# A four-layer diffusion backbone on one core: the first FFN products behind both mixers read unnormalised x, and the norm's root is applied to their results

## The chip, the core and the metric

The kernel runs on one NeuronCore of a Trainium2 chip. TensorE (PE) multiplies matrices into PSUM, VectorE (DVE) and ScalarE (ACT) work on tiles of up to 128 partitions in SBUF and PSUM, GpSimd (POOL) on tiles in SBUF, and DMA queues bring weights from HBM. Each engine works through its own instruction stream in order and waits on semaphores. The metric is the device time of one execution in microseconds; lower is better. Before the change it is 1661.69 us, the median of three runs (1661.11 to 1663.94).

## The reference

There are 256 latent tokens (`x`) and 256 context tokens (`ctx`), each 1024 wide, and two layers. A layer is a half FFN, a token mixer and a second half FFN; the mixer of layer 0 is a 2-D Fourier mixing, that of layer 1 a bidirectional retention. In the last layer the context ends with the mixer, so the second FFN of layer 1 works on latent tokens alone.

```python
def rmsnorm(x, g):
    y = x * rsqrt(mean(x * x, axis=-1, keepdims=True) + 1e-6)
    return y * g
def modulate(h, shift, scale):
    return h * (1 + scale) + shift
def swiglu(h, w_gate, w_up, w_down):
    return (silu(h @ w_gate) * (h @ w_up)) @ w_down          # 1024 -> 2816 -> 1024
def half_ffn(t, m, j):
    h = modulate(rmsnorm(t, norm_g[l, j]), m[3 * j], m[3 * j + 1])
    return t + 0.5 * m[3 * j + 2] * swiglu(h, w_gate[l, j // 2], w_up[l, j // 2], w_down[l, j // 2])
# layer: t = half_ffn(t, m, 0); t = t + m[5] * mixer(modulate(rmsnorm(t, g1), m[3], m[4])); t = half_ffn(t, m, 2)
```

The nine vectors `m` of a layer come from `silu(c) @ ada_w[l] + ada_b[l]`, once for the latent tokens and once for the context tokens. With r the root of a token (the reciprocal square root above), `h @ w = r * ((x * g * (1 + scale)) @ w) + shift @ w`. All data is fp32.

## The kernel before, in words

Everything is held transposed: features on partitions, tokens along the free axis. The model width is eight tiles of 128 features (`d` or `k` = 0 to 7); a tile's free axis is 512 tokens, of which 0 to 255 are latent (stream 0) and 256 to 511 context (stream 1). `xlat` and `xctx` hold the residual streams.

**Products.** A matrix product in near-fp32 precision is three single-pass products of split operands. Each operand is written as hi + lo (ScalarE casts hi, VectorE subtracts to get lo: `split`, L88 to L92), and `mm3` (L130 to L134) issues hi*hi, hi*lo, lo*hi into one PSUM accumulation. In the names of the profile `h` is the normalised and modulated input of an FFN or a mixer (sixteen tiles: hi and lo of eight), `wh` and `wl` are the halves of a weight block, `raw` is a block as it comes from HBM, `ps` is one of six PSUM banks and `aux` one of two more. One FFN block of 1024 x 256 weights (128 columns of gate and 128 of up) is 48 products; 22 blocks make the hidden layer, in three chunks, each followed by its share of the down projection.

**The norm.** As each tile of the residual stream is finished (`residual`, L369), ScalarE squares it (L271), and GpSimd or VectorE adds the squares up (L278). `rstd` (L297) then forms one stream's roots: products with a single column sum over partitions (L303), ScalarE takes the square root (L308), VectorE the reciprocal (L310) and a diagonal matrix (L312), and one product spreads the roots over all partitions as a row (L319). `norm_mod` (L327) makes h from it, per tile: VectorE x * scale * root (L335), ScalarE hi with the shift added (L336), VectorE lo (L337). Both read the root from PSUM.

**The two places.** Behind the Fourier mixer (`fourier`, its last loop) and behind the retention (`project_out` of the last head) the latent stream's norm must be complete before the first FFN product can be issued. `keep_warm` (L245) puts products of a constant matrix (L250) at three points of this chain. After that `begin_two` (L1084) starts the FFN of both streams: block 0 and block 1 on the 256 latent columns alone, while the context's norm is formed, then both blocks on the context columns, and from block 2 on all 512 columns at once. `begin_narrow` (L1108) starts the last FFN, which has latent columns only, with blocks 0 and 1.

**The order of the work.** The program is written as one sequence; a scheduler of the framework moves instructions within it by its own estimates, under `tc.issue_after` constraints. Within an engine the resulting order is fixed, so an instruction that waits holds up all that stand behind it on its engine.

## Time and profile before

| What | Value |
|---|---|
| Median of three runs | 1661.69 us |
| The profiled execution's own time | 1660.66 us |
| Its span, first to last instruction | 1658.6 us |
| Mean granted TensorE clock | 0.997 |
| TensorE busy | 1632.2 us, 98% of the span |
| VectorE, ScalarE, GpSimd busy | 1128.2, 627.3, 112.5 us |

The profile names instructions by line, engine, operation, result and operands. In its timelines a row holds the start, the duration, the engine, the line, the shapes and a count of equal instructions that follow each other; a bracket tells for how long the engine was idle before and who released it. Instructions of one engine overlap in part, so the step from one start to the next, and not the duration, is what an instruction costs a busy engine. A full-precision (fp32) product is two records, a split one is one.

### The profile page before, as it was taken

To read this page: it belongs to the slowest core of one execution; us is meant where nothing else is said; L and a number is where in the kernel's file an instruction comes from. 1 tells how busy PE (TensorE), PEld (TensorE's weight loads), DVE (VectorE), ACT (ScalarE), POOL (GpSimd) and SP (SyncE) were. 2 spreads that over 40 slices of the span, in tenths; PEclk is the share of its full clock that TensorE was granted. 3 is DMA by queue.
4 is the path that set the end of the run, shared out by engine and by line. 5 is a ranking of instruction groups with operands and counts; after the bars stand their busy time and mean duration, and the time that the engine had idled before them with its cause. 6 is when DMAs were issued, how large, how long until landed. Compare 5 with 4: busy or idle time off the path is not lost.

```text
span 1658.6 us, 23343 instructions
## 1 busy us (share of the span) xinstructions
PE 1632.2 (98%) x9400; PEld 1429.1 (86%) x9400; DVE 1128.2 (68%) x1805; ACT 627.3 (38%) x910; POOL 112.5 (7%) x180
## 2 busy tenths in 40 slices
PE   6999999999999999999999999999999999999998
PEld 4788888889998888888988888888998999999998
DVE  5688888887867776766566767733566757665554
ACT  4522222255542122223442232233574444354443
POOL 0001111112200000001100000001000000000000
PEclk9999999999999999999999999999999999999999
DMA  9675776752235444544144444422233334345551
GB/s 333 248 261 196 258 256 228 244 197 77 77 140 178 167 166 153 194 163 169 68 152 165 156 167 172 171 99 99 77 127 128 127 108 147 128 164 190 169 188 54
DMA packets 59740, 272.04 MB, mean 164 GB/s; under 512 B 7536, under 2 KB 8944, under 8 KB 41968
## 3 DMA queue, kind: packets, MB, share of 16 engines
q1 hardware_dynamic: 40512, 201.86, 34.4%
q0 software_dynamic: 18576, 68.17, 11.6%
q8 instruction: 74, 1.21, 0.3%
q10 hardware_dynamic: 544, 0.52, 0.1%
q14 instruction: 34, 0.28, 0.0%
HBM read 265.27 MB, written 5.24 MB: 163 GB/s over the span
## 4 chain that ended last, share of the span: by engine, by line
PE 97%; DVE 1%; DMA 1%; ACT 1%; issue 0%; SPq 0%; DVEq 0%; ACTq 0%
PE ps L132 31%; PE ps L133 31%; PE ps L134 31%; DMA a<-in_ada_first 1%; PE aux L303 1%; PE ps L764 0%; PE aux L250 0%; PE aux L195 0%; DMA xctx<-in_x 0%; PE ps L839 0%; ACT wh L89 0%; PE aux L319 0%; PE aux L925 0%; DVE xlat L369 0%; PE aux L358 0%
## 5 line engine op out<-in xcount | busy, mean ns | idle before, releaser
L89 ACT CAST wh<-raw 128x1024 fp32r<-128x1024 f32 x344 | 352.4, 1031 | 712.0 <-PE ps L133 625.9
L133 PE MATMUL ps<-h,wh 128*128 128x512 f32 (+1 forms) x1568 | 554.7, 355 | 0.0
L134 PE MATMUL ps<-h,wl 128*128 128x512 f32 (+1 forms) x1568 | 554.0, 355 | 0.0
L132 PE MATMUL ps<-h,wh 128*128 128x512 f32 (+1 forms) x1568 | 549.7, 355 | 2.5 <-ACT h L89 2.5
L90 DVE TENSOR_TENSOR wl<-raw,wh 128x1024 fp32r<-128x1024 f32 x344 | 410.0, 1197 | 180.1 <-ACT wh L89 175.6
L133 PEld LDWEIGHTS ps<-h,wh 128*128 128x128 f32 x1568 | 296.3, 189 | 41.8 <-DVE h L90 0.4
L132 PEld LDWEIGHTS ps<-h,wh 128*128 128x128 f32 x1568 | 293.6, 189 | 44.5 <-ACT h L89 3.1
L222 DVE CUSTOM_DVE_ANT_0 dump<-araw,wide,adab 128x1024 bf16<-128x1024 f32 x256 | 329.4, 1287 | 3.7 <-DMA araw<-in_ada_w 0.4
L134 PEld LDWEIGHTS ps<-h,wl 128*128 128x128 f32 x1568 | 296.2, 189 | 41.0
L132 PE MATMUL ps<-a,wh 128*128 128x512 f32 (+2 forms) x952 | 317.9, 337 | 0.0
L133 PE MATMUL ps<-a,wh 128*128 128x512 f32 (+2 forms) x952 | 317.9, 336 | 0.0
L134 PE MATMUL ps<-a,wl 128*128 128x512 f32 (+2 forms) x952 | 317.6, 336 | 0.0
L133 PEld LDWEIGHTS ps<-a,wh 128*128 128x128 f32 x952 | 180.8, 190 | 18.8
L134 PEld LDWEIGHTS ps<-a,wl 128*128 128x128 f32 x952 | 180.7, 190 | 18.3
L132 PEld LDWEIGHTS ps<-a,wh 128*128 128x128 f32 x952 | 180.1, 190 | 18.6
L439 DVE TENSOR_TENSOR t<-ps,t 128x512 f32<-128x512 f32 (+1 forms) x88 | 54.9, 624 | 175.3 <-PE ps L134 147.8
L213 POOL DMA_DIRECT2D araw<-in_ada_w x128 | 67.9, 531 | 828.9 <-DVE mods L222 777.8
L369 DVE SCALAR_TENSOR_TENSOR xlat<-ps,mods,xlat 128x256 f32<-128x256 f32 x128 | 61.1, 480 | 63.6 <-PE ps L134 63.0
L437 ACT ACTIVATE t<-ps 128x512 f32<-128x512 f32 (+1 forms) x88 | 48.0, 545 | 130.7 <-PE ps L134 125.0
L90 DVE TENSOR_TENSOR a<-t,a 128x512 fp32r<-128x512 f32 (+2 forms) x116 | 69.8, 606 | 2.4 <-ACT a L89 2.0
L89 ACT CAST a<-t 128x512 fp32r<-128x512 f32 (+2 forms) x116 | 64.2, 558 | 12.0 <-DVE t L868 9.1
L278 POOL TENSOR_TENSOR q<-q,q 128x256 f32<-128x256 f32 x40 | 36.9, 940 | 188.9 <-ACT q L271 188.7
(208 smaller groups left out, 1159.6 us busy)
## 6 DMA issues: line engine op xcount, KB each, us to landing
raw<-in_wgu SPq DMA_DIRECT2D x85, 1024.0 KB, 4.8
araw<-in_ada_w POOLq DMA_DIRECT2D x128, 512.0 KB, 3.8
raw<-in_wd SPq DMA_DIRECT2D x32, 896.0 KB, 4.5
raw<-in_ret_in SPq DMA_DIRECT2D x24, 1024.0 KB, 4.8
raw<-in_wd SPq DMA_DIRECT2D x16, 1024.0 KB, 4.8
a<-in_ada_first SPq DMA_DIRECT2D x32, 256.0 KB, 5.2
t<-in_four_w SPq DMA_DIRECT2D x32, 256.0 KB, 5.2
raw<-in_ret_out SPq DMA_DIRECT2D x8, 1024.0 KB, 4.7
```

Source lines behind the costliest of these rows:

```text
L89: mark[6] = nc.scalar.copy(hi, src)
L90: i = (lo_eng or nc.vector).tensor_tensor(lo, src, f32(hi), ALU.subtract)
L132: nc.tensor.matmul(ps, lh, rh, start=start, stop=False)
L133: nc.tensor.matmul(ps, lh, rl, start=False, stop=False)
L134: mark[4] = nc.tensor.matmul(ps, ll, rh, start=False, stop=stop)
L213: nc.gpsimd.dma_start(raw, a["ada_w"][l, m, d])
L222: nc.vector.tensor_tensor_reduce(dump, raw, wide[:, v, :], 1.0, adab[:, l, m, d : d + 1], ALU.mult, ALU.add, mods[l][:, m, d, v : v + 1],)
L278: eng.tensor_tensor(n, sums[s][0], sq, ALU.add)
L303: mark[5] = nc.tensor.matmul(ps[:, t : t + 1], sq[:, t * P : t * P + P], meanw[:, 0:1], start=(i + t == 0), stop=(i == n - 1), skip_group_ ...
L369: mark[0] = nc.vector.scalar_tensor_tensor(x_tile(d, s), ps, mods[l][:, m, d, s : s + 1], x_tile(d, s), ALU.mult, ALU.add)
L437: mark[1] = nc.scalar.activation(sg[:, :width], psg[:, :width], AF.Silu)
L439: nc.vector.tensor_tensor(hf[:, :width], psu[:, :width], sg[:, :width], ALU.mult)
```

## The change

Behind both mixers, the first FFN blocks no longer read normalised tiles for the latent tokens.

As each residual tile d is finished, `Ahead.tile(d)` writes x * g * (1 + scale), without the root, as hi and lo into the latent columns of the FFN's h tiles (ScalarE hi, VectorE lo). Each h tile is two columns wider (`SH = 2`): columns 0 and 1 hold the shift vector, hi and lo, written by GpSimd in `Ahead.open()`. A product over columns 0 to 257 then gives, in one pass, the shift's product (column 0) and the unnormalised products of the 256 latent tokens. When the roots are known, `evict` multiplies columns 2 to 257 by the root row as VectorE moves them out of PSUM, and `gate` adds the shift's product as a bias per partition inside the Silu and the gating product.

The squares of both streams are now all added by GpSimd, down to one tile for each stream, and behind the Fourier mixer the roots of both streams are formed in one chain (`roots`), whose first products stand between the FFN products. The `keep_warm` products and the two separate `rstd` chains at these places go. Behind the Fourier mixer blocks 0 and 1 are computed so for the latent tokens, then both for the context columns, which are normalised as before; behind the retention blocks 0, 1 and 2 are. Meanwhile `norm_mod` overwrites the latent columns with normalised values for the other blocks, once the last unnormalised product has read them.

All h tiles have the new width, so every FFN and mixer product that reads h starts two columns (8 bytes) into its tile.

```diff
     def h_tile():
-        return hpool.tile([P, 512], F32R, tag="h", name=nm("h"))
+        return hpool.tile([P, SH + T2], F32R, tag="h", name=nm("h"))
...
     def h_tiles():
-        return [(h_tile(), h_tile()) for _ in range(ND)]
+        return [(h_tile()[:, SH:], h_tile()[:, SH:]) for _ in range(ND)]
...
@@ fourier, last loop
                 for s in range(2):
                     residual(d, z[:, STREAMS[s]], l, 5, s)
-                    square(d, s, nc.gpsimd, 2)
-                    if d == ND - 1 and s == 0:
-                        sqrt_table()
-                        keep_warm(NW[0], mark[4])
-                        after(0)
-        after(1)
+                    if s == 0:
+                        following.tile(d)
+                for s in (1, 0):
+                    square(d, s)
+        sqrt_table()
...
@@ retention, project_out of the last head
                     if hd == HEADS - 1:
-                        square(d, 0, nc.vector, 2)
+                        following.tile(d)
+                        square(d, 0)
...
+        following.open()
         project_out(HEADS - 1, zts.pop(0))
-        keep_warm(NW[0], mark[4])
-        after(0)
...
+    class Ahead:
...
+        def open(self):
+            need(self.l, 3 * self.j + 1)
+            self.full = [(h_tile(), h_tile()) for _ in range(ND)]
...
+            for d, (hi, lo) in enumerate(self.full):
+                sh = mods[self.l][:, 3 * self.j, d, 0:1].broadcast_to([P, SH])
+                nc.gpsimd.tensor_copy(hi[:, :SH], sh)
+                nc.gpsimd.tensor_tensor(lo[:, :SH], sh, f32(hi[:, :SH]), ALU.subtract)
+
+        def tile(self, d):
+            sc = mods[self.l][:, 3 * self.j + 1, d, 0:1]
+            hi, lo = (t[:, STREAMS[0]] for t in nxt["h"][d])
+            nxt["done"][1].append(nc.scalar.activation(hi, x_tile(d, 0), AF.Copy, scale=sc))
+            mark[0] = nc.vector.scalar_tensor_tensor(lo, x_tile(d, 0), sc, f32(hi), ALU.mult, ALU.subtract)
...
+        def products(self, blk, ps, k):
+            hi, lo = (t[:, : SH + S] for t in self.full[k])
+            for gu in range(2):
+                mm3(
+                    ps[gu][:, : SH + S], wcols(blk, k // 4 * 1024 + gu * 512 + k % 4 * P, P), (hi, lo),
+                    k == 0, k == ND - 1,
+                )
+
+        def evict(self, ps, r):
+            col = spool.tile([P, 2], F32, tag="col", name=nm("col"))
+            v = []
+            for gu in range(2):
+                nc.vector.tensor_copy(col[:, gu : gu + 1], ps[gu][:, 0:1])
+                v.append(q_tile())
+                nc.vector.tensor_tensor(v[gu], ps[gu][:, SH : SH + S], r, ALU.mult)
+            return v, col
+
+        def gate(self, v, col, pair):
+            uh, ul = pair
+            sg = q_tile()
+            mark[1] = nc.scalar.activation(sg, v[0], AF.Silu, bias=col[:, 0:1])
+            hf = q_tile()
+            nc.vector.scalar_tensor_tensor(hf, v[1], col[:, 1:2], sg, ALU.add, ALU.mult)
+            split(uh[:, :S], ul[:, :S], hf)
+
+        def roots(self, n):
+            inv = rstd_tokens(n, 1.0 / D**2)
+            diag = t_tile()[:, : n * S]
...
+            r = aux_tile()
+            for s in range(n):
+                nc.tensor.matmul(r[:, STREAMS[s]], meanw, diag[:, STREAMS[s]], start=True, stop=True)
+            row = q_tile()
+            nc.scalar.copy(row, r[:, :S])
+            return r, row
+
+        def begin_two(self, load, bank, part, hidden):
...
+            for k in range(ND):
+                self.products(blks[0], lat[0], k)
+                if k == 4:
+                    r, row = self.roots(2)
+            nxt["done"] = norm_mod(self.l, self.j, 1, h, r[:, late])
+            with behind(3):
+                first = self.evict(lat[0], row)
+            for k in range(ND):
+                self.products(blks[1], lat[1], k)
+            with behind(ND - 1):
+                second = self.evict(lat[1], row)
+                pre = [load(2)]
+            ctx = [(bank(), bank()) for _ in range(2)]
+            for k in range(ND):
+                for i in range(2):
+                    for gu in range(2):
+                        part(blks[i], ctx[i][gu], gu, (k,), late)
+                if k == 0:
+                    with tc.issue_after(mark[0].ins), tc.issue_after(mark[6].ins):
+                        nxt["done"] = norm_mod(self.l, self.j, 0, h, r[:, :S])
...
+        def begin_narrow(self, load, bank, part, hidden):
...
+            for k in range(ND):
+                self.products(blks[0], lat[0], k)
+                if k == 4:
+                    r, row = self.roots(1)
...
-    fourier(0, 0, prepare(0, 2, T2, True))
-    half_ffn(0, 2, nxt["h"], T2, begin_two, prepare(1, 0, T2))
+    following = Ahead(0, 2)
+    fourier(0, 0, following)
+    half_ffn(0, 2, nxt["h"], T2, following.begin_two, prepare(1, 0, T2))
...
-    retention(1, 0, nxt["h"], late, prepare(1, 2, S, True))
-    half_ffn(1, 2, nxt["h"], S, begin_narrow, finish, scale_out)
+    following = Ahead(1, 2)
+    retention(1, 0, nxt["h"], late, following)
+    half_ffn(1, 2, nxt["h"], S, following.begin_narrow, finish, scale_out)
```

Where the instructions stand now, at three places. Rows give line, operation, result and operands with the buffers' numbers, and the result's shape; in the changed program `mm3` is L134 to L136, the tile's lo L1049, the sums over partitions L360, the spreading product L1088.

**TensorE between the Fourier mixer's last product and the FFN.** Before:

```order
L134 MATMUL ps_4056<-a_3409,wl_4014 128x258
L250 MATMUL aux_4094<-meanw 128x128 x6
L303 MATMUL aux_4117<-meanw,q_4000 128x1 x2
L303 MATMUL aux_4117<-meanw,q_4051 128x1 x2
L303 MATMUL aux_4117<-meanw,q_4090 128x1 x2
L250 MATMUL aux_4130<-meanw 128x128 x5
L319 MATMUL aux_4136<-q_4128,meanw 128x256
L250 MATMUL aux_4138<-meanw 128x128 x5
L303 MATMUL aux_4233<-meanw,q_4005 128x1 x2
L303 MATMUL aux_4233<-meanw,q_4054 128x1 x2
L132 MATMUL ps_4189<-h_4101,wh_4181 128x256
```

Now, at the same place (first rows) and 75 products later, inside block 1 (last rows):

```order
L136 MATMUL ps_4106<-a_3409,wl_4058 128x258
L134 MATMUL ps_4163<-h_3743,wh_4155 128x258
L135 MATMUL ps_4163<-h_3744,wh_4155 128x258
...
L134 MATMUL ps_4166<-h_3751,wh_4173 128x258
L360 MATMUL aux_4207<-meanw,q_4145 128x1 x2
L136 MATMUL ps_4165<-h_3751,wl_4174 128x258
L135 MATMUL ps_4166<-h_3752,wh_4173 128x258
L360 MATMUL aux_4207<-meanw,q_4149 128x1 x2
L136 MATMUL ps_4166<-h_3751,wl_4174 128x258
```

FFN products follow the mixer's last product at once; q_4145 and q_4149 are GpSimd's last sums of squares of the context and the latent stream. The products that spread the roots stand behind the last product of block 1, and the context's products right behind them:

```order
L136 MATMUL ps_4166<-h_3757,wl_4174 128x258
L1088 MATMUL aux_4218<-t_4216,meanw 128x256 x2
L134 MATMUL ps_4345<-h_3743,wh_4155 128x256
L134 MATMUL ps_4346<-h_3743,wh_4155 128x256
L135 MATMUL ps_4345<-h_3744,wh_4155 128x256
```

Before, the context was normalised while block 1 ran on the latent columns; now its first product stands directly behind its roots.

**VectorE at the end of the Fourier mixer, now.** The evictions (L681 to L683), residuals (L371), lo halves (L1049), and the two halves of block 1's weights (L92):

```order
L681 TENSOR_TENSOR t_4135<-ps_4106,t_4120 128x2x128
L682 TENSOR_TENSOR t_4135<-ps_4106,t_4120 128x2x128
L371 SCALAR_TENSOR_TENSOR xlat<-t_4090,mods_126,xlat 128x256
L371 SCALAR_TENSOR_TENSOR xctx_98<-t_4090,mods_126,xctx_98 128x256
L683 COPY t_4135<-ps_4106 128x2
L371 SCALAR_TENSOR_TENSOR xlat<-t_4135,mods_126,xlat 128x256
L371 SCALAR_TENSOR_TENSOR xctx_98<-t_4135,mods_126,xctx_98 128x256
L1049 SCALAR_TENSOR_TENSOR h_3756<-xlat,mods_126,h_3755 128x256
L1049 SCALAR_TENSOR_TENSOR h_3758<-xlat,mods_126,h_3757 128x256
L92 TENSOR_TENSOR wl_4170<-raw_4167,wh_4169 128x1024
L92 TENSOR_TENSOR wl_4174<-raw_4167,wh_4173 128x1024
L367 RECIPROCAL inv_4214<-root_4212 128x4
```

Eight lo halves are new in this stretch; the last two (tiles 6 and 7) stand behind the last residuals.

**TensorE behind the retention, now.** Block 0 begins directly behind the mixer; the sums of squares stand after its 48 products and two of block 1:

```order
L136 MATMUL ps_12686<-h_12479,wl_12682 128x258
L134 MATMUL ps_12687<-h_12465,wh_12693 128x258
L135 MATMUL ps_12687<-h_12466,wh_12693 128x258
L360 MATMUL aux_12741<-meanw,q_12673 128x1 x2
...
L135 MATMUL ps_12687<-h_12478,wh_12697 128x258
L1088 MATMUL aux_12750<-t_12748,meanw 128x256
L136 MATMUL ps_12687<-h_12477,wl_12698 128x258
```

The product that spreads the roots stands 36 products later, and behind it the blocks go on with unnormalised tiles.

More of the change, by code (lines that the diff above doesn't have):

```diff
@@ L32 @@
 GRID_W = 64
+SH = 2
 @with_exitstack
@@ L333, in norm_mod @@
             hi, lo = h[d][0][:, sl], h[d][1][:, sl]
-            with tc.issue_after(done[d - 3].ins) if d > 2 else nullcontext():
+            with tc.issue_after(done[-3].ins) if len(done) > 2 else nullcontext():
                 nc.vector.scalar_tensor_tensor(u, x_tile(d, s), sc, r, ALU.mult, ALU.mult)
@@ L350, in scale_parts, with rstd_tokens @@
         return each
-    def rstd_tokens():
+    def rstd_tokens(n=2, scale=1.0):
         ps = aux_tile()
-        for s in range(2):
+        for s in reversed(range(n)):
             for t in range(2):
@@ L708, in rsqrt_small, with retention @@
         return y
-    def retention(l, slot, h, mid, after):
+    def retention(l, slot, h, mid, following):
         need(l, NMOD - 1)
```

87 lines of the change are left out of this document (62 added, 25 removed).

## The prediction

> **What bounds the kernel now.** I read the page's head and busy times first, then the chain of waits, then TensorE's timeline at the two places of the change.
>
> ```profile
> span 1658.6 us, 23343 instructions
> PE 1632.2 (98%) x9400; PEld 1429.1 (86%) x9400; DVE 1128.2 (68%) x1805; ACT 627.3 (38%) x910; POOL 112.5 (7%) x180
> ...
> PE 97%; DVE 1%; DMA 1%; ACT 1%; issue 0%; SPq 0%; DVEq 0%; ACTq 0%
> ```
>
> TensorE is the bound: 1632.2 of 1658.6 us, and 97% of the chain that ended last. But busy is not useful here, since the constant products of L250 count as busy. So the price of a junction is the time from the mixer's last product to a point where both programs have done the same FFN products, less what these need at the steady step. The timeline of TensorE behind the Fourier mixer:
>
> ```profile
> 427.28 0.28 PE L668 MATMUL ps<-a,a 96*128 96x258 f32 x1
> 430.28 0.28 PE L668 MATMUL ps<-a,a 96*128 96x258 f32 x1
> ...
> 443.84 1.50 PE L250 MATMUL aux<-meanw 128*128 128x128 f32 x12
> 445.18 1.65 PE L303 MATMUL aux<-meanw,q 128*128 128x1 f32 x12
> 448.00 0.67 PE L319 MATMUL aux<-q,meanw 128*128 128x256 f32 x2
> 449.94 1.02 PE L303 MATMUL aux<-meanw,q 128*128 128x1 f32 x8
> 450.82 0.48 PE L132 MATMUL ps<-h,wh 128*128 128x256 f32 x2
> ...
> 474.80 0.40 PE L132 MATMUL ps<-h,wh 128*128 128x512 f32 x1
> ```
>
> The step: 25 products lie between the first two rows, 13 of 258 columns and 12 of 256, in 3.00 us, so 0.12 us each. From 443.84 to 450.82 nothing useful is multiplied. From 443.84 to the first 512-wide product at 474.80 are 30.96 us; blocks 0 and 1, both streams, are 4 x 48 = 192 products or 23.04 us. **Junction 1 costs 7.92 us.** Behind the retention:
>
> ```profile
> 1452.60 1.50 PE L250 MATMUL aux<-meanw 128*128 128x128 f32 x12
> 1454.29 1.47 PE L303 MATMUL aux<-meanw,q 128*128 128x1 f32 x12 [0.19 <-DVE q L278]
> 1456.86 0.67 PE L319 MATMUL aux<-q,meanw 128*128 128x256 f32 x2
> 1457.36 1.28 PE L250 MATMUL aux<-meanw 128*128 128x128 f32 x10
> 1458.64 0.74 PE L132 MATMUL ps<-h,wh 128*128 128x256 f32 x4
> 1459.28 0.39 PE L133 MATMUL ps<-h,wh 128*128 128x256 f32 x1
> 1459.50 0.28 PE L134 MATMUL ps<-h,wl 128*128 128x256 f32 x1
> ```
>
> 6.04 us to the first product, and its first five take 0.86 us (1458.64 to 1459.50) where 0.60 is the steady step: **junction 2 costs 6.30 us.** Together 14.22 us can be touched; the rest of the program keeps its products.
>
> **The change, part by part.** The number and the width of the other products stay. A product of 258 columns costs no more than one of 256, as the mixed step above shows, so 96 of them at junction 1 and 144 at junction 2 are free.
>
> *Junction 2, what stays.* The sum over partitions is now one tile, two rows of L303's kind, four records. Eight records took 0.88 us (449.94 to 450.82), so 0.44. One spreading product took 0.50 (1456.86 to 1457.36). Sum 0.94, gain 6.30 - 0.94 = **5.36 us**. That holds if no wait is left. The lo halves come while the mixer still runs; the last is needed seven tiles of six products, 5 us, after the mixer's end. The sums stand after 50 products, 6.0 us after it. Before, VectorE's last square sum landed at 1454.29, 1.7 us after the mixer's end; GpSimd's adds are slower, but six of the seven can run earlier. I take no wait.
>
> *Junction 1, what stays.* Row sums of two streams: eight records, 0.88 us. Two spreading products, 1.00 us. Then a new wait. The context's first product now stands directly behind the spreading products, so TensorE waits for VectorE's x * scale * root and ScalarE's hi. That wait is seen at junction 2 before, where it is filled with L250: from the end of the spreading product (1457.36) to 1458.64, 1.28 us, and 0.26 of slow start, 1.54. ScalarE's copy of the root row stands ahead of it:
>
> ```profile
> L802 ACT COPY t<-ps 128x256 f32<-128x256 f32 x8 | 3.0, 372 | 1.2 <-DVE t L797 1.1
> 450.36 0.47 DVE L335 SCALAR_TENSOR_TENSOR q<-xlat,mods,aux 128x256 f32<-128x256 f32 x1
> 451.15 0.48 DVE L335 SCALAR_TENSOR_TENSOR q<-xlat,mods,aux 128x256 f32<-128x256 f32 x1
> ```
>
> 0.37 more: 1.9 us. After it VectorE makes a tile in 0.79 us (450.36 to 451.15), while block 0's six products of a tile need 0.72: over six tiles 0.4 us.
>
> *The clock.* L250 held TensorE busy; what does a bare wait cost? The windows of two microseconds, with the granted clock third from the end, and the timeline ahead of them:
>
> ```profile
> 414.92 0.39 PE L132 MATMUL ps<-a,t 128*128 128x256 f32 x1 [0.70 <-ACT t L89]
> 415.14 0.28 PE L133 MATMUL ps<-a,t 128*128 128x256 f32 x1
> 416.23 0.39 PE L134 MATMUL ps<-a,t 128*128 128x256 f32 x1 [0.80 <-DVE t L90]
> ...
> 416.00:418.00 2.00, 1.77 (x11) 1.72 (x12) 1.94 (x9) 0.81 (x3) 0.00 (x0) 0.78 0.00 0
> 418.00:420.00 2.00, 2.00 (x11) 2.00 (x11) 0.86 (x4) 0.79 (x3) 0.00 (x0) 0.50 0.00 0
> 420.00:422.00 2.00, 2.00 (x17) 2.00 (x17) 0.73 (x3) 0.89 (x3) 0.00 (x0) 0.86 0.00 0
> ```
>
> Two waits of 0.70 and 0.80 us, with two products between them, were followed by half the clock: (0.22 + 0.50 + 0.14) x 2 = 1.7 us lost. One wait of nearly the same sum was not:
>
> ```profile
> 48.20 1.66 PE L132 MATMUL ps<-h,wh 128*128 128x512 f32 x6 [1.62 <-ACT h L89]
> ...
> 48.00:50.00 2.00, 1.80 (x7) 1.25 (x8) 2.00 (x4) 2.00 (x5) 0.00 (x0) 1.00 0.99 418
> ```
>
> So the loss sets in somewhere from 1.5 to over 1.6 us. The wait of 1.9 us and the gaps of the pace behind it, 2.3 us, lie above both: I count 1.7 us, and keep 0 as the other end.
>
> The Trainium skill, "TensorE: Matmul & The Clock Gate", section "Why this matters for your kernels", allows more: no idle gaps over about 3 us. By it the sum would be 1.7 us lower; the loss behind 1.5 us at 414 to 416 contradicts it.
>
> *The new work on VectorE.* Eight lo halves fall into the mixer's last loop, where VectorE has no room:
>
> ```profile
> 425.00:446.00 21.00, 21.00 (x179) 21.00 (x177) 20.33 (x44) 12.11 (x27) 9.62 (x10) 1.00 0.43 151
> 445.58 0.48 DVE L369 SCALAR_TENSOR_TENSOR xctx<-t,mods,xctx 128x256 f32<-128x256 f32 x1
> L348 DVE SCALAR_TENSOR_TENSOR h<-xlat,mods,h 128x256 fp32r<-128x256 f32 x8 | 5.7, 716 | 1.1 <-ACT h L347 1.0
> ```
>
> It is busy 20.33 of 21.00 us, and its last residual ends at 446.06. The same instruction (L348) took 716 ns in the mean beside GpSimd's adds; alone the step is 0.40 (two such instructions in 0.79 us, above). So the last lo comes 8 x 0.40 to 8 x 0.72 later, at 449.3 to 451.8; tile 7 needs it at 443.84 + 7 x 0.72 + 0.24 = 449.12. TensorE waits 0.2 to 2.7 us. I take 0.7, near the lower end, since GpSimd is busy in only 9.62 of the 21 us and the earlier lo halves can fill the 0.67 us idle. Block 1's weights (L92, behind it) and the roots' reciprocal come later by the same time and have 5 us of products ahead of them.
>
> ScalarE's eight hi halves lie beside this (12.11 of 21.00 us busy). GpSimd's 32 small shift writes come before its adds, behind 42.78 us of idle (row below). The later normalisation of the latent columns and the gates (some 24 instructions of about 0.40 on VectorE) lie beside block 2's 48 wide products, 11 us. No queue of DMAs gains or loses a transfer, and the modulation steps (L222) keep their places in VectorE's order, though `open` asks for them earlier.
>
> Junction 1 then keeps 0.88 + 1.00 + 1.9 + 0.4 + 1.7 + 0.7 = 6.6 us, gain 7.92 - 6.6 = **1.3 us**. Bounds: without the clock, the late lo and the pace 4.1; with the late lo at 2.7 and a second loss of clock, -2.4.
>
> *The start of h tiles.* All products over h now start 8 bytes into a tile.
>
> ```profile
> L133 PE MATMUL ps<-h,wh 128*128 128x512 f32 x1056 | 411.1, 389 | 0.0
> 499.76 0.39 PE L134 MATMUL ps<-h,wl 128*128 128x512 f32 x1
> 501.34 0.39 PE L132 MATMUL ps<-h,wh 128*128 128x512 f32 x1
> ```
>
> Of the 512-wide ones there are 3 x 1056 = 3168 (this line and its neighbours L132, L134). No row shows such a start. The lower end is 0, since the odd width above cost nothing; the upper what two columns of 512 would be, 0.9 ns of the step (seven from 499.76 to 501.34, 226 ns each), or 2.8 us; I take 0.
>
> **Sum.** 5.4 + 1.3 = 6.7 us off the profiled execution's 1660.66: 1654.0. The median of three runs was 1.0 above that execution, so I predict **1655.0 us**.
>
> **Rivals.** *Sums late.* GpSimd now adds all fourteen squares, in a chain that TensorE meets in the middle of block 1:
>
> ```profile
> 433.12 2.35 DVE L90 TENSOR_TENSOR wl<-raw,wh 128x1024 fp32r<-128x1024 f32 x2
> 433.66 2.40 POOL L278 TENSOR_TENSOR q<-q,q 128x256 f32<-128x256 f32 x1 [42.78 <-ACT q L271]
> L278 POOL TENSOR_TENSOR q<-q,q x40: 729/785/2405, 375.6 to 1180.6; 128x256 f32<-128x256 f32 x40
> ```
>
> An add of 729 ns lasted 2.40 us beside VectorE's two weight halves, and just such a pair (L92) now stands behind the last lo. If four adds are left at its end (lo at 449.8 by the sum, 2.3 for the pair, 0.79 an add), 449.8 + 2.3 + 4 x 0.79 = 455.3, against the row sums' place at 443.84 + 75 x 0.12 + 0.7 = 453.5: 1.8 us more, 1656.8. Beside it, lo halves at their late bound add 2.0: 1657.0. Against it: VectorE's idle moments in the last loop let GpSimd in. The Trainium skill, "SBUF — State Buffer", section "Who interferes with whom", says that a VectorE instruction with two SBUF inputs and a GpSimd one that reads SBUF exclude each other; the 2.40 us row agrees, and by it the wait would be the 1.8 us worked out here.
>
> *The clock stays.* The wait at the context is one piece like that of 1.62 us, not two, and may fall across whatever stretch the clock is judged by: 1655.0 - 1.7 = 1653.3. The rule of the Trainium skill's page on the clock gate, quoted above, speaks for this one.
>
> *Moved, not removed.* Late lo (2.0) and late sums (1.8) together leave 2.9 of the 6.7 us: 1658.8; with a second loss of clock (1.7) 1660.5. For it: both hang on the same full VectorE. Against it: late lo halves also delay block 1, and so give the sums time. No change, by what can be measured.
>
> *Slower.* One mechanism: the shifted start costs each wide product. From 6.7 / 3168 = 2.1 ns each the change gains nothing; were it 16 columns of 512, 7.1 ns, it would be 22.5 us and 1677.5. Against it: the 258-wide products end at an odd place at no cost.
>
> **How the numbers follow.** Forecast 0.37 (1654 to 1656); clock stays 0.25 (1653.3); sums or lo late 0.22 (1657); moved 0.09 (1658.8 to 1660.5); slower 0.05; that the gain at junction 2 is lost in another way 0.02. Two runs of this kernel can be told apart by about 0.2%, 3.3 us. Faster needs 1658.4 or less: 0.84; same 0.10; slower 0.06. Range 1651.8 to 1659.5.
>
> **What would show it.** Right: no L250 at either place, the first FFN product 0.1 to 0.2 us behind the mixer's last, TensorE waiting at the context's first product for ScalarE's hi for about 2 us, a clock of about 0.5 in the next 3 us, and no wait behind the retention. Wrong: a wait of over 1 us at the row sums (L360) on GpSimd's add; waits for L1049's lo over 1 us; a step of the 512-wide products other than 226 ns.

## The result, and the profile after

| | Median | Executions | Lowest to highest |
|---|---|---|---|
| before | 1661.40 us | 4 | 1660.31 to 1663.94 |
| changed | 1675.20 us | 4 | 1674.44 to 1679.17 |

The ratio is 1.0087, with a 95% interval of 1.0075 to 1.0098: the change makes the kernel 13.8 us slower. I had predicted 1655.0 us. The profiled execution is the one of 1679.17 us. Its mean granted clock is 0.994; the other three have 0.998 and spans of 1672.3 to 1673.3 us, so about 4 us of its span are not the change's.

The head of the page after, as before in one line each for span and TensorE:

```profile
span 1677.0 us, 23316 instructions
PE 1647.7 (98%) x9312; PEld 1426.0 (85%) x9312; DVE 1139.4 (68%) x1838; ACT 632.2 (38%) x931; POOL 131.0 (8%) x223
```

TensorE has 88 records fewer than before and is busy 15.5 us longer. Where, the groups by line and shape tell. Of the kernel before (columns behind the shapes: count, busy us, mean ns of one, idle just before):

```profile
L134 PE MATMUL ps<-h,wl 128*128 128x512 f32 x1056 | 410.9, 389 | 0.0
L132 PE MATMUL ps<-h,wh 128*128 128x512 f32 x1056 | 409.8, 390 | 2.5 <-ACT h L89 2.5
L132 PE MATMUL ps<-a,wh 128*128 128x512 f32 x472 | 183.7, 389 | 0.0
L132 PE MATMUL ps<-wh,h 128*128 128x512 f32 x64 | 25.2, 393 | 0.0
L132 PE MATMUL ps<-wh,a 128*128 128x512 f32 x64 | 24.9, 390 | 0.0
```

And of the changed kernel, where `mm3` stands at L134 to L136:

```profile
L136 PE MATMUL ps<-h,wl 128*128 128x512 f32 x1056 | 419.3, 397 | 0.0
L135 PE MATMUL ps<-h,wh 128*128 128x512 f32 x1056 | 418.8, 397 | 0.4 <-DVE h L92 0.4
L134 PE MATMUL ps<-h,wh 128*128 128x512 f32 x1056 | 415.6, 396 | 1.8 <-ACT h L91 1.8
L134 PE MATMUL ps<-a,wh 128*128 128x512 f32 x472 | 183.8, 389 | 0.0
L134 PE MATMUL ps<-wh,h 128*128 128x512 f32 x64 | 25.4, 396 | 0.0
L134 PE MATMUL ps<-wh,a 128*128 128x512 f32 x64 | 24.9, 390 | 0.0
```

The three groups of wide products over h were 411.1 (shown in the prediction), 410.9 and 409.8 us, 1231.8 in all; now they are 1253.7. That is 21.9 us more, at the same count, while the wide products over the hidden layer's tiles (`a`) did not change. The two rows with `wh` first are from the retention, where weights stream and h is the stationary operand: those with h grew from 393 to 396 ns, those with `a` kept 390. So whatever meets an h tile in a wide product pays. The step, from two rows of the timeline with 52 products between their starts:

```profile
499.49 0.39 PE L135 MATMUL ps<-h,wh 128*128 128x512 f32 x1
...
511.67 0.39 PE L136 MATMUL ps<-h,wl 128*128 128x512 f32 x1
```

12.18 us by 52 are 234 ns, where the prediction had 226.

The junctions did what was forecast. Behind the Fourier mixer (timeline of TensorE):

```profile
451.69 0.28 PE L136 MATMUL ps<-a,wl 128*128 128x258 f32 x1
451.81 0.29 PE L134 MATMUL ps<-h,wh 128*128 128x258 f32 x1
...
457.28 0.36 PE L135 MATMUL ps<-h,wh 128*128 128x258 f32 x1 [0.72 <-DVE h L1049]
...
465.47 1.03 PE L1088 MATMUL aux<-t,meanw 128*128 128x256 f32 x4
468.07 0.51 PE L134 MATMUL ps<-h,wh 128*128 128x256 f32 x2 [1.57 <-ACT h L338]
...
481.68 0.39 PE L134 MATMUL ps<-h,wh 128*128 128x512 f32 x1
```

From the first FFN product (451.81) to the first wide one (481.68) are 29.87 us, less 192 x 0.12: **junction 1 costs 6.83 us**, 1.1 less than the 7.92 before. The clock behind the wait of 1.57 us, in windows of two microseconds (third from the end):

```profile
468.00:470.00 2.00, 1.80 (x11) 1.58 (x12) 2.00 (x6) 1.46 (x5) 0.00 (x0) 0.95 0.00 0
470.00:472.00 2.00, 2.00 (x12) 2.00 (x11) 2.00 (x8) 1.39 (x3) 0.00 (x0) 0.50 0.00 0
472.00:474.00 2.00, 2.00 (x14) 2.00 (x14) 2.00 (x6) 1.64 (x3) 0.00 (x0) 0.70 0.00 0
```

Behind the retention, in the timeline of before, the first product of the down projection, and of the changed kernel the first FFN product, the row sums and again the first product of the down projection:

```profile
1504.97 0.28 PE L132 MATMUL ps<-a,wh 128*128 128x256 f32 x1
```

```profile
1475.20 0.28 PE L134 MATMUL ps<-h,wh 128*128 128x258 f32 x1
...
1481.21 0.50 PE L360 MATMUL aux<-meanw,q 128*128 128x1 f32 x4
...
1522.14 0.28 PE L134 MATMUL ps<-a,wh 128*128 128x256 f32 x1
```

384 FFN products lie in both stretches. Before it took 1504.97 - 1452.60 = 52.37 us, now 1522.14 - 1475.20 = 46.94: **5.4 us gained at junction 2**, and no wait is left. The balance: 1661.4 - 5.4 - 1.1 + 21.9 = 1676.8, against 1675.2 measured. The question for the chip was what makes a wide product 7 ns longer.

### The profile page after: what moved, and what is told of

It is laid out like the page before. It is cut to its first block, busy times and chain, and to the rows that moved or that the text cites. A ratio compares the mean times of both kernels' runs of the same rounds, so it can differ in the third digit from the quotient of the medians.

```text
span 1677.0 us, 23316 instructions
## 1 busy us (share of the span) xinstructions
PE 1647.7 (98%) x9312; PEld 1426.0 (85%) x9312; DVE 1139.4 (68%) x1838; ACT 632.2 (38%) x931; POOL 131.0 (8%) x223
## 4 chain that ended last, share of the span: by engine, by line
PE 94%; DVE 2%; DMA 2%; ACT 1%; issue 0%; SPq 0%; DVEq 0%; ACTq 0%
PE ps L136 31%; PE ps L135 31%; PE ps L134 30%; DMA a<-in_ada_first 1%; DVE wl L92 1%; PE ps L768 0%; DMA raw<-in_wgu 0%; DMA xctx<-in_x 0%; PE aux L305 0%; ACT wh L91 0%; PE ps L843 0%; DVE h L1049 0%; DVE xlat L371 0%; DVE xctx L371 0%; PE aux L360 0%
## 5 line engine op out<-in xcount | busy, mean ns | idle before, releaser
L135 PE MATMUL ps<-h,wh 128*128 128x512 f32 (+2 forms) x1568 | 562.8, 360 | 1.3 <-DVE h L1049 0.7
L136 PE MATMUL ps<-h,wl 128*128 128x512 f32 (+2 forms) x1568 | 563.1, 361 | 0.0
L134 PE MATMUL ps<-h,wh 128*128 128x512 f32 (+2 forms) x1568 | 556.4, 359 | 3.4 <-ACT h L91 1.8
L92 DVE TENSOR_TENSOR wl<-raw,wh 128x1024 fp32r<-128x1024 f32 x344 | 411.1, 1201 | 173.2 <-ACT wh L91 167.8
L134 PEld LDWEIGHTS ps<-h,wh 128*128 128x128 f32 x1568 | 294.5, 189 | 51.1 <-ACT h L91 2.4
L136 PEld LDWEIGHTS ps<-h,wl 128*128 128x128 f32 x1568 | 297.3, 190 | 45.9
L134 PE MATMUL ps<-a,wh 128*128 128x512 f32 (+2 forms) x952 | 318.1, 337 | 0.0
L136 PE MATMUL ps<-a,wl 128*128 128x512 f32 (+2 forms) x952 | 317.8, 336 | 0.0
L136 PEld LDWEIGHTS ps<-a,wl 128*128 128x128 f32 x952 | 180.2, 190 | 18.5
L134 PEld LDWEIGHTS ps<-a,wh 128*128 128x128 f32 x952 | 179.5, 190 | 18.8
L371 DVE SCALAR_TENSOR_TENSOR xlat<-ps,mods,xlat 128x256 f32<-128x256 f32 x128 | 61.1, 480 | 65.6 <-PE ps L136 64.9
L92 DVE TENSOR_TENSOR a<-t,a 128x512 fp32r<-128x512 f32 (+2 forms) x113 | 68.0, 606 | 1.9 <-ACT a L91 1.6
L280 POOL TENSOR_TENSOR q<-q,q 128x256 f32<-128x256 f32 x51 | 47.6, 950 | 219.4 <-ACT q L273 216.2
```

The source lines that it names most:

```text
L92: i = (lo_eng or nc.vector).tensor_tensor(lo, src, f32(hi), ALU.subtract)
L134: nc.tensor.matmul(ps, lh, rh, start=start, stop=False)
L135: nc.tensor.matmul(ps, lh, rl, start=False, stop=False)
L136: mark[4] = nc.tensor.matmul(ps, ll, rh, start=False, stop=stop)
L280: eng.tensor_tensor(n, sums[s][0], sq, ALU.add)
L371: mark[0] = nc.vector.scalar_tensor_tensor(x_tile(d, s), ps, mods[l][:, m, d, s : s + 1], x_tile(d, s), ALU.mult, ALU.add)
```

## The experiments

**Is it the start, and of what kind?** Four kernels with other starts. In the first three the only edit to the kernel before is n = 2, 4 or 8 in

```diff
-        return hpool.tile([P, 512], F32R, tag="h", name=nm("h"))
+        return hpool.tile([P, n + T2], F32R, tag="h", name=nm("h"))[:, n:]
```

The build rounds such tiles up to 2080 bytes. *start8*:

> The kernel before with one edit: h tiles two columns wider, data from column 2, nothing else of the change. Theory A (the start 8 bytes into the tile is what costs): from 499.72 to 511.90 us the changed kernel makes 52 wide products, 234 ns each, against 227; 7 ns x 3168 = 22 us, so the step of the 512-wide products over h is 234 ns here too, and the time 1661.4 + 22 = 1683 us (1680 to 1687). Rival B (the start is harmless, and the wide products are slowed by something else in the change, by other engines' traffic or the clock): step 227 ns, time 1661 us.

1684.06 us (1681.24 to 1686.78), ratio 1.0138 (1.0123 to 1.0154). Two columns ahead of the data, with nothing else of the change, cost 22 us:

```profile
L134 PE MATMUL ps<-h,wl 128*128 128x512 f32 x1056 | 418.6, 397 | 0.0
L133 PE MATMUL ps<-h,wh 128*128 128x512 f32 x1056 | 418.1, 396 | 0.1
L132 PE MATMUL ps<-h,wh 128*128 128x512 f32 x1056 | 415.4, 395 | 2.5 <-ACT h L89 2.5
```

> The kernel before, with h data 16 bytes into each tile (tiles lie 2080 bytes apart, as with 8). If A holds and only the place of a start in a line of 64 or 32 bytes counts: step 234 ns, about 1683 us. If A holds and a start that is a multiple of 16 bytes is good enough: 227 ns, 1661 us. Rival B: 1661 us.

One execution: 1668.10 us, before 1661.92.

> The kernel before, with h data 32 bytes into each tile; tiles again lie 2080 bytes apart, so that half of the data starts at a multiple of 64 bytes and half at 32. It parts the start from the spacing of the tiles. If a line of 32 bytes counts: 227 ns, 1661 us. If a line of 64 counts: 227 and 234 ns in turn by tile, 1672 us. If the spacing of 2080 bytes is the cause and not the start: 234 ns, 1683 us.

One execution: 1671.17 us. Here I missed: a start at a multiple of 32 bytes is no cure, and 16 bytes cost less than 32. *aligned* is the changed kernel with 16 columns ahead, the shift in the last two:

> The changed kernel, with 14 unused columns ahead of the two shift columns: data starts 64 bytes into each tile, the 258-wide products 56 bytes in. Theory A: the wide products are back at 227 ns, the junctions keep their gain (first FFN product 0.12 us behind the mixer's last at both), and the time is 1675.2 - 22 = 1653 us (1649 to 1656), faster than both kernels by 0.3% to 0.7%. The 258-wide products, which still start off a boundary, stay at 0.12 us a step. Rival B: 1675 us as the changed kernel.

1666.70 us (1665.98 to 1668.30), ratio 1.0030 (1.0019 to 1.0042). All data starts at a multiple of 64 bytes, and still the wide products take 231 ns. Theory A, that only the 8 bytes count, fell here. In these four kernels and in the changed one the tiles lie 2080 or 2112 bytes apart, so that their starts fall at different places within 256 bytes; in the kernel before they lie 2048 apart, all at one place. In the trace of *start32* the mean step, sorted by a product's position in its block of 48, runs from 227.5 to 234.8 ns and repeats every twelve products, as the places of the h tiles modulo 256 bytes do.

**Equal places.** *even8* is the kernel before with tiles 2304 bytes apart (9 x 256) and data 8 bytes in:

```diff
+        return hpool.tile([P, 64 + T2], F32R, tag="h", name=nm("h"))[:, 2 : 2 + T2]
```

> The kernel before with h tiles 2304 bytes apart (64 unused columns in each) and data again 8 bytes into each tile, so that every tile starts at the same place within 256 bytes. In the runs so far the step of a wide product follows the places, modulo 256 bytes, of its own moving tile and of its two neighbours'. Theory C (unequal places of successive moving tiles are the cost, not the 8 bytes): step 226.7 ns, 1661.9 us as the kernel before. Theory A as first put (a start 8 bytes off a boundary costs by itself): 233 ns, 1683 us.

One execution: 1680.91 us, step 233 ns. Theory C fell as well: equal places among the h tiles don't help if the place is 8. *even256* is the changed kernel with 64 columns ahead (256 bytes), which puts all data at place 0 (and with one buffer in place of four for a one-column tile on ScalarE):

> The changed kernel with 62 unused columns ahead of the shift columns, tiles 2304 bytes apart, so that all data starts at the same place within 256 bytes as before. Theory C: all 3168 wide products at 226.7 ns, and only the junctions' gain is left. From the changed kernel 1675.2 - 3168 x 6.6 ns = 1654.3 us; from the run with 64 bytes ahead 1666.7 - 3168 x 4.4 ns = 1652.8 us: I expect 1653.5 (1651.5 to 1655.5). If the spacing isn't the cause: 1666 us or more.

1653.53 us (1651.61 to 1655.29), ratio 0.9950 (0.9937 to 0.9962), and the wide products are back:

```profile
L136 PE MATMUL ps<-h,wh 128*128 128x512 f32 x1056 | 411.5, 390 | 0.2 <-DVE h L93 0.2
L137 PE MATMUL ps<-h,wl 128*128 128x512 f32 x1056 | 411.5, 390 | 0.1
L135 PE MATMUL ps<-h,wh 128*128 128x512 f32 x1056 | 410.2, 390 | 3.7 <-ACT h L92 3.7
```

So the change itself, with its data at the old place, is 8 us faster than before (7.9 by the medians, 6.3 to 10.5 by the interval). What was left was what the place is measured against.

**Against the weights.** In *h64* an unused tile of 64 bytes stands ahead of the h tiles and one of 192 behind them, so that the rest keeps its places; in *all64* only the one ahead, so that hidden tiles and weights move along; in *weights64* the 64 bytes stand ahead of the weights' pool alone. *h128* and *h32* are *h64* with 128 and 32 bytes.

```diff
+    gap1 = ctx.enter_context(tc.tile_pool(name="gap1", bufs=1))
     hpool = ctx.enter_context(tc.tile_pool(name="hpool", bufs=16))
+    gap2 = ctx.enter_context(tc.tile_pool(name="gap2", bufs=1))
     apool = ctx.enter_context(tc.tile_pool(name="apool", bufs=22))
```

> The kernel before with all h tiles moved by 64 bytes (64 unused bytes ahead of them, 192 behind, so that everything else keeps its place modulo 256 bytes). Tiles stay 2048 bytes apart, so successive moving tiles start at equal places, on a 64-byte boundary, but 64 bytes off the weights' places modulo 256. Theory D (what costs is a moving tile that starts at another place modulo 256 bytes than the weights it meets): step of the 512-wide h products above 229 ns, time above 1668 us. Theory E (a start off a 64-byte boundary costs, and unequal neighbours cost, the weights play no part): 226.7 ns, 1661.5 us.

> The kernel before with the same 64 bytes ahead of the h tiles and nothing taken back behind them: the h tiles, the hidden layer's tiles and the weights all move by 64 bytes together. Theory D: all relations are as before, step 226.7 ns, 1661.5 us. If what counts is the place modulo 256 bytes in itself: step above 229 ns for the h products and for those over the hidden layer's tiles (1416 products) too, time above 1670 us. Theory E: 1661.5 us.

> The kernel before with 64 unused bytes ahead of the weights' tiles alone: the h tiles and the hidden layer's tiles keep their places, the weights (and what lies behind them) move by 64 bytes. Theory D (the moving tile's place relative to the weights that are loaded beside it): now both kinds of wide products pay, those over h (3168) and those over the hidden layer's tiles (1416), 229 ns or more, 2.2 ns x 4584 = 10 us, about 1671 us. Rival F (the partner is not the weights but another tile that moved with them in the run all64): 226.7 ns, 1661.5 us.

> As h64 with 128 bytes: the h tiles alone, all at 128 modulo 256. Theory D with a cost that falls with the distance (6.6 ns at 8 bytes, 2.2 at 64): 2 ns or less, 1661.5 to 1668 us. Theory D with any unequal place alike: 229 to 231 ns, 1668 to 1675 us.

> As h64 with 32 bytes. Between 8 bytes (6.6 ns) and 64 (2.2 ns): about 4 ns, 1674 us, if the cost falls with the distance. If every unequal place on a 32-byte boundary costs alike: 229 ns, 1668 us.

The groups of *weights64*, over h, over hidden tiles, and in the retention with hidden tiles stationary:

```profile
L135 PE MATMUL ps<-h,wh 128*128 128x512 f32 x1056 | 417.8, 396 | 0.0
L135 PE MATMUL ps<-a,wh 128*128 128x512 f32 x472 | 185.7, 395 | 0.0
L134 PE MATMUL ps<-wh,a 128*128 128x512 f32 x64 | 25.4, 398 | 0.0
```

All three are longer, where only the weights moved; and in *all64* (next), where everything moved together, none is:

```profile
L135 PE MATMUL ps<-h,wh 128*128 128x512 f32 x1056 | 411.9, 390 | 0.0
L134 PE MATMUL ps<-a,wh 128*128 128x512 f32 x472 | 183.7, 389 | 0.0
L134 PE MATMUL ps<-wh,a 128*128 128x512 f32 x64 | 24.9, 390 | 0.0
```

Rival F and theory E fell, theory D stands. The table holds the place of the h tiles, modulo 256 bytes, relative to the weights (from the addresses of the build), the mean distance between the starts of successive records over the whole trace in ns (without the distances above 300 ns for wide products and 130 ns for 256-wide ones, which hold a wait or a slower clock), and the time with that of before beside it.

| Kernel | Place | wide, h | wide, hidden | 256-wide, h | Time (before), us |
|---|---|---|---|---|---|
| before | 0 | 226.8 | 226.7 | 119.9 | 1661.40 |
| even256 | 0 | 226.8 | 226.7 | 119.9 | 1653.53 (1661.42) |
| all64 | 0, all moved | 226.8 | 226.7 | 119.9 | 1665.62 (1662.40) |
| even8 | 8 | 233.4 | 226.8 | 118.7 | 1680.91 (1661.42) |
| h32 | 32 | 233.3 | 226.9 | 117.3 | 1678.51 (1661.23) |
| h64 | 64 | 229.0 | 226.9 | 117.8 | 1668.47 (1662.40) |
| h128 | 128 | 233.2 | 226.8 | 118.7 | 1678.55 (1661.23) |
| weights64 | 192, hidden too | 233.3 | 233.3 | 114.2 | 1673.42 (1661.23) |
| start16 | 16 + 32k, mixed | 230.1 | 226.8 | 117.6 | 1668.10 (1661.92) |
| start32 | 32k, mixed | 231.2 | 226.8 | 118.3 | 1671.17 (1661.92) |
| start8 | 8 + 32k, mixed | 233.4 | 226.9 | 119.7 | 1684.06 (1661.92) |
| changed | 8 + 32k, mixed | 233.4 | 226.9 | 119.7 | 1675.20 (1661.40) |
| aligned | 64k, mixed | 231.2 | 226.8 | 118.3 | 1666.70 (1661.92) |

The cost does not simply fall with the distance, as I had expected for *h128* and *h32*: 64 is the cheap place, 8, 32, 128 and 192 cost alike. The single execution of *all64* lies 3.2 us above its before at equal steps; its trace has a wait for a ScalarE cast of 3.40 us, at 51.00 us, where the trace of the kernel before has one of 1.62 (at 48.20), and its mean clock is 0.996 against 0.997, which is 1.7 us more.

**The other sign.** *weights64* lost 12 us, though its wide products lost 6.5 x 3168 + 6.6 x 1416 = 30 us. The last column but one tells why: products of 256 columns became shorter, 114.2 ns against 119.9, which is 17 us for 2976 of them. The 1671 us that I had expected came close by luck: it counted a loss of 10 us and no gain. Two kernels put only these at unequal places. *last192* is the kernel before with h and hidden tiles of the last FFN, which has no wide products, from column 48 on:

```diff
+                if width == S:
+                    h[:] = [(hi[:, 48:], lo[:, 48:]) for hi, lo in h]
...
+                if width == S:
+                    uh, ul = uh[:, 48:], ul[:, 48:]
```

> The kernel before, with one edit in the last FFN, which has only 256-wide products: its h tiles and its hidden tiles are written and read from column 48 on, 192 bytes off the weights' place modulo 256. In the run weights64, where every tile stood at 192, a 256-wide product took 114.1 ns against 120 at equal places (and a 512-wide one 233 against 227). Theory D with both signs: 1584 products x 5.8 ns = 9.2 us less, 1652.5 us. Rival: the shorter step of weights64 hangs on something else that moved there: 1661.5 us.

1651.94 us, ratio 0.9951 (0.9933 to 0.9969). 50 us of the last FFN, before and in *last192* (fourth entry: TensorE's busy time and instructions):

```profile
1500.00:1550.00 50.00, 50.00 (x419) 50.00 (x419) 27.88 (x35) 21.41 (x28) 0.00 (x0) 1.00 0.50 172
```

```profile
1500.00:1550.00 50.00, 50.00 (x443) 50.00 (x442) 29.95 (x37) 22.66 (x29) 0.00 (x0) 1.00 0.52 185
```

443 products in place of 419; from start to start they take 113.3 ns in the mean, in place of 120.0. Four lines gain 9.7 us by the medians, which is no less than the whole change at the junctions (7.9 in *even256*; the intervals overlap).

**The junctions apart.** *only2* is *even256* with junction 1 as before.

> The kernel even256 with the junction behind the Fourier mixer as it was before (its two root chains, the constant products, both streams normalised first); only the junction behind the retention is changed. It measures the two junctions apart. By the prediction's terms the one behind the retention gains 5.4 us: 1661.9 - 5.4 = 1656.5 us, and the other 1.3 us, so even256 would be 1.3 us faster than this. Rival (from the changed kernel's trace: the distance from the retention's last product to the end is only 4.2 us shorter): 1657.7. If the whole gain of about 8 us seen after taking off the wide products' cost lies behind the retention: 1654.

1656.42 us (1655.47 to 1658.81), ratio 0.9969 (0.9957 to 0.9982): 5.0 us for junction 2, where 5.4 was forecast, and 2.9 us between it and *even256* for junction 1, with intervals that allow the 1.3 forecast. They allow the rival's 1657.7 us as well, so that the 5.4 us rest on the trace above. *warm* keeps the clock at junction 1:

```diff
             ctx = [(bank(), bank()) for _ in range(2)]
+            keep_warm(12, self.spread)
```

> The kernel even256 with 12 constant products (128 columns, 0.13 us each, 1.6 us) put into the wait ahead of the context's first product behind the Fourier mixer. In the changed kernel that wait was 1.57 us and the granted clock fell to 0.5 and 0.7 in the four microseconds after it. If the wait costs the clock: no window below 0.9 there and 1.6 us less than even256. If the clock falls for another reason: same time as even256, or up to 0.3 us more.

1652.28 us (1651.44 to 1655.11), ratio 0.9948 (0.9936 to 0.9961). The total does not show a gain over *even256*, since the intervals overlap. The windows at the place, of *even256* (first) and of *warm*:

```profile
462.00:464.00 2.00, 2.00 (x12) 2.00 (x11) 2.00 (x8) 1.18 (x3) 0.00 (x0) 0.50 0.00 0
```

```profile
460.00:462.00 2.00, 2.00 (x20) 2.00 (x19) 2.00 (x6) 1.46 (x5) 0.00 (x0) 1.00 0.00 0
462.00:464.00 2.00, 2.00 (x19) 2.00 (x18) 2.00 (x8) 1.43 (x3) 0.00 (x0) 1.00 0.00 0
```

The clock of 0.50 is 1.00 here. The twelve products have two records each and lasted 2.6 us, not the 1.6 expected, and so filled 1 us more than the wait. By the first FFN product and the first wide one (443.91 and 472.56, 444.44 and 474.15 in *even256*), junction 1 costs 5.61 us instead of 6.67. That is 1.1 us gained, although the context's first product came 0.9 us later behind the spreading products. That the filling is what kept the clock is not shown. *aligned* has the same wait, unfilled, and kept its clock too:

```profile
464.01 0.51 PE L135 MATMUL ps<-h,wh 128*128 128x256 f32 x2 [1.57 <-ACT h L339]
```

```profile
464.00:466.00 2.00, 1.86 (x12) 1.63 (x13) 2.00 (x6) 1.46 (x4) 0.00 (x0) 1.00 0.00 0
466.00:468.00 2.00, 2.00 (x17) 1.82 (x15) 2.00 (x8) 1.34 (x3) 0.00 (x0) 1.00 0.00 0
```

So the same wait cost the clock in two executions and not in a third. From this row to the first wide product *aligned* takes 12.4 us (to 476.40) and *even256* 13.5 (460.64 to 474.15), where the 96 products need 11.5: the kept clock is worth 1.1 us and not 1.7, since at full clock more of VectorE's slower pace shows. *spread7* and *spread6* shorten the wait instead:

```diff
             for k in range(ND):
-                self.products(blks[1], lat[1], k)
+                with tc.issue_after(self.spread.ins) if k >= LATE else nullcontext():
+                    self.products(blks[1], lat[1], k)
```

> The kernel even256 with the two spreading products of the roots ahead of the last six latent products of block 1 instead of behind them. In even256 TensorE waited 1.57 us behind the spreading products, and the clock fell to half for 3 us after it (1.7 us lost). Six products are 0.73 us: the wait becomes 0.84 us if the diagonal is there in time, and the clock stays: 0.7 + 1.7 = 2.4 us less than even256, 1651.1 us. If the clock falls at 0.84 us too: 0.7 us less.

> As spread7, with twelve products (1.46 us) behind the spreading products. The wait behind block 1 falls to 0.1 us; if VectorE's diagonal comes too late by then, up to 0.5 us of it comes back ahead of the spreading products. 1.1 to 1.5 + 1.7 us less than even256: 1650.5 us, at most 0.5 from spread7.

1653.35 us (1651.57 to 1653.93), ratio 0.9945 (0.9932 to 0.9957), and 1655.50 us (1652.73 to 1658.99), ratio 0.9959 (0.9947 to 0.9971). In the trace of *spread7* the wait is as forecast, and the windows behind it keep the clock:

```profile
459.46 0.51 PE L136 MATMUL ps<-h,wh 128*128 128x256 f32 x2 [0.87 <-ACT h L340]
```

```profile
460.00:462.00 2.00, 1.90 (x14) 1.87 (x15) 2.00 (x7) 1.23 (x3) 0.00 (x0) 1.00 0.00 0
462.00:464.00 2.00, 2.00 (x17) 1.83 (x16) 2.00 (x9) 1.27 (x3) 0.00 (x0) 1.00 0.04 8
```

Junction 1 is down to 4.9 us (443.97 to 471.95, less 23.04), 1.7 less than in *even256*, where 2.4 were expected: behind the wait the 96 products of the context again took 12.5 us (459.46 to 471.95). In *spread6* the wait is 0.15 us, and 0.34 us come back ahead of the spreading products, as expected. The medians do not show these 1.7 us: the intervals of *even256*, *spread7* and *spread6* overlap, and their profiles lose different amounts of clock at other places (0.95 and 0.90 between 400 and 435 us in *spread7* and *spread6*). So the shorter wait is shown in place, and its gain in the total is not; that it is what kept the clock is open, after *aligned*.

**Both together.** *narrow192* is *spread7* with the last FFN's tiles at 192:

> The kernel spread7 (the changed kernel, wide products at equal places, spreading products earlier), with the last FFN's h and hidden tiles at 192 modulo 256 relative to the weights. 1440 products of 256 columns x 5.8 ns = 8.4 us less than spread7 (1653.4): 1645 us, 1.0% faster than before. Rival: 1653 us.

1650.04 us (1648.43 to 1650.83), ratio 0.9924 (0.9912 to 0.9936): the lowest median of all (its interval touches that of *last192*), 0.8% faster than before, but 5 us short of what I expected. The last FFN's steps tell where these 5 us went, and not why:

```profile
1500.00:1550.00 50.00, 50.00 (x427) 50.00 (x426) 28.48 (x36) 22.13 (x28) 0.00 (x0) 1.00 0.52 182
```

427 products are 117.8 ns a step, where *last192* had 113.3 at the same place. The products over h take this long, and those over hidden tiles as well, though hidden tiles and weights have the same spacing and the same distance from each other as in *last192* (by the addresses of the build). One difference is that the weights lie 4096 bytes further from the h tiles:

> The kernel last192 with 4096 unused bytes ahead of the weights' tiles, which keeps every place modulo 256 (and 4096) and moves the weights as far as the wider h tiles do in narrow192. In last192 the 256-wide products of the last FFN took 113.3 ns a step, in narrow192, at the same 192, 117.6. If the distance between tiles and weights above 4096 bytes sets the size: 117.6 ns here, 1651.9 + 1584 x 4.3 ns = 1658.7 us. If it doesn't, and the h tiles' spacing or another tile does: 113.3 ns, 1651.9 us.

One execution: 1652.17 us, 443 products in the same window, 113.3 ns. So the distance of 4096 bytes is not it. What makes 117.8 of 113.3 stays open; for products of 256 columns the place relative to the weights is not all that counts.

## Why the prediction was wrong

- **The step that failed** is "The start of h tiles", which I put at 0 with 2.8 us as its upper bound. It is 6.6 ns for each of 3168 products, 20.9 us by the steps and 21.9 by the groups. The bound came from the 258-wide products, which end at an odd column at no cost. That row could not bound it: it is about a width, not a start, and at half the width the effect has the other sign (products of 256 columns: 119.9 ns, and 118.7 at place 8). The prediction's own sign of being wrong, a step of the wide products other than 226 ns, is what the trace shows.
- **The rival "Slower"** named the mechanism, its point of decision (2.1 ns) and, with 7.1 ns, nearly its size; 1677.5 us against 1675.2. I gave it 0.05. Its size was a guess ("16 columns"), and what decides is not the start in itself but its place relative to the weights, which no row of before could show, since there every place was 0.
- **Junction 2**: 5.36 us forecast, 5.4 in the trace, 5.0 in *only2*. No wait was left, as argued.
- **Junction 1**: 1.3 us forecast, 1.1 in the trace. The late lo waits 0.72 us (0.7 forecast), the context's first product 1.57 (1.9), and the clock loses (0.05 + 0.50 + 0.30) x 2 = 1.7 us (1.7). That the clock's term came out is partly luck: with the same wait *aligned* lost nothing, and gained only 1.1 us by that, because the pace (0.4 forecast) grows when the clock stays: the two terms don't simply add. The clock term's basis does not hold either: the pair of waits of 0.70 and 0.80 us, which the prediction saw followed by half the clock, stands in *weights64* too (423.82 and 425.12 us), and the clock there stayed at 1.00.
- **"The clock stays"** (0.25) is out in the profiled executions of the changed kernel and of *even256*, and came true in *aligned*, at the same 1.57 us. The prediction's bound, a loss that sets in "from 1.5 to over 1.6 us", is no threshold: in *even256* a wait of 2.60 us (at 49.62 us) was followed by none. The Trainium skill, "TensorE: Matmul & The Clock Gate", section "Why this matters for your kernels", allows gaps up to about 3 us; the windows at 0.50 behind 1.57 us contradict it.
- **"Sums late"** and **"moved"**: the row sums wait for no GpSimd sum at either place. The one row of TensorE that names such a sum is the weight load at 457.25 us (0.90 us), which belongs to the product of the late lo and its 0.72 us; behind the retention the row sums (1481.21 us) come 6.0 us after the first FFN product, as forecast.
- **The sum**: 6.7 us of gain forecast, 7.9 in *even256* (1661.42 to 1653.53), which has the tiles' place and the small buffer apart from the changed kernel. Its 1653.5 us lie in my range; the changed kernel does not.

## What to carry to other kernels

A change of a tile's width moves the starts of all tiles in its pool, and of all pools behind it; in these runs a wide matrix product kept its 227 ns only while the streamed tile and the weights loaded beside it started at the same place modulo 256 bytes. So, for wide products, pad to a multiple of 256 bytes (or take the extra columns from elsewhere; for 256-wide products equal places were the slow ones), and compare the mean duration of the untouched groups before and after: 389 against 397 ns, in a group that the change did not mean to touch, pointed to the answer. Before such a term is set to 0, ask whether the row that bounds it has the same shape and the same thing varied.

## What the runs showed of the hardware

- A product of 512 columns, with the next weights loaded beside it, steps at 226.7 ns if moving tile and weights start at equal places modulo 256 bytes, and at 229.0 (64) to 233.4 ns (8, 32, 128, 192) if not. That holds for either operand: in the retention the weights stream, h is loaded, and the same rows grow. Which place is cheap differs there: with the weights streaming, 64 bytes past the loaded hidden tiles, the step went from 227.2 to 233.4 ns (*weights64*). A product's own weights and the next one's, loaded beside it, have the same place in all runs, so that the two are not told apart.
- Products of 256 columns behave the other way: 119.9 ns at equal places, 113.3 to 119.7 at unequal ones; 113.3 is half of 226.7, and the same 192 bytes gave 113.3 (*last192*) and 117.8 (*narrow192*). Why the signs differ was not tested.
- The Trainium skill, "TensorE: Matmul & The Clock Gate", section "Step-by-step: what each phase is for", says that loading the next weights doesn't steal SBUF read bandwidth from the running product. At equal places nothing here speaks against it (226.7 ns with a load beside every product; no run has a wide product without one); at unequal ones the 6.6 ns of *h32* and *weights64*, which change nothing but places, speak against it. That the two reads meet in the same part of SBUF is a guess; only the places were varied.
- A wait of 1.57 us on TensorE was followed by half the clock for about 3 us in the changed kernel and in *even256*, and by no loss in *aligned*; one of 2.60 us in *even256* and one of 0.87 us in *spread7* by none. The length of the wait alone does not decide, and what else does was not tested.
